# Sixteen block sums of the output weights moved from GpSimd to VectorE

## The chip, the core and the metric

The kernel runs on one core of one Trainium2 chip. The metric is the time of one execution in device microseconds (us), and lower is better. The core has five engines with a queue each: TensorE (PE in the profile, its weight loads PEld), VectorE (DVE), ScalarE (ACT), GpSimd (POOL) and SyncE (SP), which here only issues DMAs. Every engine takes its instructions in order. PSUM is the memory into which TensorE writes; GpSimd works on SBUF alone in this kernel.

## The reference

One layer of a block with two parallel branches, 1024 tokens of width 1024 and 256 context tokens, all in float32:

```python
h  = rms_norm(x, g_pre) * (1 + sc) + sh
ua, gate_a, q, k, v, gate_b, gm = split_proj(h @ w_in)
...                                   # rms norm and rotary on q and k, context keys and values appended
o  = latent_attention(q, k_all, v_all)            # 16 heads, 4 key groups, softmax over 1280 keys
y_attn = (o * silu(gate_b)) @ w_attn_out
y_conv = conv_module(ua, gate_a, ...)             # 31 taps, layer norm, silu, @ w_conv_out
out = (sigmoid(ga) * y_conv + sigmoid(gb) * y_attn) @ w_out
x_new = x + gt * rms_norm(out, g_post)
```

What matters here is the last product, `@ w_out`, a 1024 x 1024 by 1024 x 1024 product.

## The kernel before

Every float32 product is made as three products of a high and a low part (`mm3`): the high part is a cast to the tensor engine's rounded float32, the low part is the rest. `split` makes the pair, with the cast on ScalarE and the subtraction on VectorE unless other engines are named.

The two products at the end (`w_attn_out`, side 0, and `w_out`, side 1) are not made as eight block products of a 2 x 2 blocking but as seven, after Winograd's form of Strassen's method. For that the weights' blocks have to be added and subtracted first. `LEFT` and `RIGHT` list these sums: an entry `(n, i, (x, op, y))` says that operand n is made in block i, as block x plus or minus block y. `right_operands` does it for `w_out`, in four rounds t = 0 to 3. In each round it loads two row strips of 128 x 1024 into tiles of the tag `y4` (three buffers; the profile calls them `y`), so that there are four blocks of 128 x 512, b[0] to b[3], two in each tile. Five operands come of them, the entries j = 0 to 4 of `RIGHT`; the first is a plain block, the other four are sums made in place: b0 = b1 - b0, b1 = b3 - b1, b3 = b3 - b0 and b2 = b2 - b3. For each operand ScalarE casts the high part (`his`, line 664), VectorE subtracts the low part (`los`, line 656), and SP stores both to DRAM (`stores`, line 658), from where `coef_load` fetches them for the product. `RSTEPS` says in which of nine steps each of these parts is issued, and how many steps of the attention loop pass before the next.

The rounds run inside the attention loop (lines 1482 to 1515), as a generator: each turn of the loop issues one step, of some 1.9 us. In a turn TensorE makes the scores of a key block (`score`, tiles `ps`), ScalarE exponentiates them (`pe`), GpSimd adds the exponentials up into `psum`, VectorE adds every fifth pair (`part`, which GpSimd then adds to `psum`), and TensorE weighs the values (`po`, 20 products in a row). Ahead of that the row maxima of the next head pair are found: TensorE makes the scores once more in `max_pieces`, VectorE reduces them (`mx`, then `mc` in `max_cols`), TensorE transposes the result and ScalarE writes it as a row (`mr`). Score tiles, maxima tiles and transposes share five PSUM buffers. Beside all that, `filler` runs the projections in small pieces (tiles `ppj`): here those of `w_conv_out`, which VectorE evicts to `ts`.

Order: TensorE's instructions stay in the order in which they are written. Those of VectorE, ScalarE and GpSimd are held to it only until line 1435; in the attention loop a scheduler orders them by priority and by when it expects their inputs. What the generators issue is marked as urgent and, on VectorE, is put behind the newest maximum:

```python
        for g in late.pop(i, []):
            with tc.issue_after(crit[0].ins), urgent():
                d = next(g, None)
```

(`crit[0]` is the newest reduction of a maximum, an instruction of VectorE; `issue_after` orders instructions of that engine alone.)

The edge column: the convolution (`conv_taps`, long before the attention loop) copies one column at the end of `odd_end`, line 809: `V.tensor_copy(O[:, 511:512], acc[:, 1, 511:512])`.

Of the kernel before, what the change touches and what calls it, by code (L numbers as in the profile page):

```python
# [34 lines left out]
def block_kernel(ctx: ExitStack, tc: tile.TileContext, x, cx, cc, wmod, bmodT, bmodg, vecs, gpost,  # L35
# [18 lines left out]
    PE, V, S, G = (Ordered(e) for e in (nc.tensor, nc.vector, nc.scalar, nc.gpsimd))  # L54
# [11 lines left out]
    def tl(tag, shape, bufs, dtype=F32, pool="sb"):  # L66
        return pools[pool].tile(list(shape), dtype, tag=tag, bufs=bufs, name=nm(tag))
# [37 lines left out]
    def f32(ap):  # L105
        return ap.bitcast(F32)
# [537 lines left out]
    def right_operands():  # L644

        for t in range(4):
            b = []
            for r in range(2):
                y = tl("y4", (P, 2, 512), 3)
                SP.dma_start(out=y[:].rearrange("p c n -> p (c n)"), in_=wout[(t + 4 * r) * P:(t + 4 * r + 1) * P, :])  # L650
                b += [y[:, c, :] for c in range(2)]
            yield 2
            w = {}
            for n, (sums, his, los, stores, rest) in enumerate(RSTEPS):
                for j in los:
                    V.tensor_tensor(out=w[j][:, 1, :], in0=b[RIGHT[j][1]], in1=f32(w[j][:, 0, :]), op=SUB)
                for j in stores:
                    SP.dma_start(out=opD[1][RIGHT[j][0]][t][:], in_=f32(w[j][:]))
                for j in sums:
                    i, (x, op, y) = RIGHT[j][1:]  # L660
                    G.tensor_tensor(out=b[i], in0=b[x], in1=b[y], op=op)
                for j in his:
                    w[j] = tl("acc", (P, 2, 512), 2, F32R) if (5 * t + j) % 3 else tl("ysum", (P, 2, 512), 1, F32R)
                    S.copy(w[j][:, 0, :], b[RIGHT[j][1]])
                yield rest
# [473 lines left out]
    def last_split():  # L1139
        yield from z_split(1)  # L1140
        yield from right_operands()
# [481 lines left out]
```

## Time and profile before

| | us |
|---|---|
| median of 3 runs | 1394.6 |
| lowest and highest | 1391.34, 1399.88 |
| the profiled execution | 1392.78 |
| span of its instructions | 1391.0 |
| TensorE busy | 1347.2 (97%) |
| VectorE busy | 1018.9 (73%) |
| GpSimd busy | 712.7 (51%) |
| ScalarE busy | 564.6 (41%) |

The span is from the first to the last instruction; the profiled execution's own time is 1.8 us longer. A helper that keeps the program's order records most instructions, so nearly all of them carry the line 50 (L50) in the profile, and one goes by the tiles' names: `y<-y,y` is an instruction that writes a tile y and reads two tiles y. In the rows of instructions in order of time the columns are the start, the duration (both in us), the engine, the line, the operation, the tiles, the shapes and the count; in square brackets stands how long the engine had been idle before it and what ended that. In the rows by stretch, each engine's busy time (and instructions) follow one another: PE, PEld, DVE, ACT, POOL, then the granted clock of TensorE, the share of the DMA engines and GB/s.

### The profile page before, as it was taken

To read this page: it belongs to the slowest core of one execution; us is meant where nothing else is said; L and a number is where in the kernel's file an instruction comes from. 1 tells how busy PE (TensorE), PEld (TensorE's weight loads), DVE (VectorE), ACT (ScalarE), POOL (GpSimd) and SP (SyncE) were. 2 spreads that over 40 slices of the span, in tenths; PEclk is the share of its full clock that TensorE was granted. 3 is DMA by queue.
4 is the path that set the end of the run, shared out by engine and by line. 5 is a ranking of instruction groups with operands and counts; after the bars stand their busy time and mean duration, and the time that the engine had idled before them with its cause. 6 is when DMAs were issued, how large, how long until landed. Compare 5 with 4: busy or idle time off the path is not lost.

```text
span 1391.0 us, 19520 instructions
## 1 busy us (share of the span) xinstructions
PE 1347.2 (97%) x6520; PEld 999.8 (72%) x6520; DVE 1018.9 (73%) x1521; ACT 564.6 (41%) x1389; POOL 712.7 (51%) x577
## 2 busy tenths in 40 slices
PE   5999999999999999999999999999999999999995
PEld 3767898988888888666666666666666665788774
DVE  3477988897979899657765776677586676348977
ACT  5542344434353442244434444544454344122232
POOL 2121346667657562346764655566446667263623
PEclk9999999999999999999999999999999999999998
DMA  9731534544544448524544444545365567699754
GB/s 342 254 122 54 183 115 132 191 140 130 174 136 153 148 130 234 169 92 157 163 144 124 150 152 127 169 130 160 99 190 190 193 207 261 202 321 352 250 183 151
DMA packets 153333, 242.45 MB, mean 174 GB/s; under 512 B 19936, under 2 KB 72716, under 8 KB 153232
## 3 DMA queue, kind: packets, MB, share of 16 engines
q1 hardware_dynamic: 139792, 218.07, 47.4%
q10 hardware_dynamic: 13440, 23.14, 5.8%
q8 instruction: 51, 0.84, 0.3%
q14 instruction: 50, 0.41, 0.1%
HBM read 161.50 MB, written 79.52 MB: 173 GB/s over the span
## 4 chain that ended last, share of the span: by engine, by line
PE 79%; DVE 6%; DMA 5%; ACT 4%; POOL 3%; issue 2%; ACTq 1%; SPq 0%; POOLq 0%; DVEq 0%
PE ppj L50 37%; PE po L50 21%; PE ps L50 17%; PE pm L50 4%; DVE t L50 2%; DMA wm<-in_wmod 1%; ACT pe L50 1%; DVE pconv L50 1%; POOL y L50 1%; DVE mx L50 1%; DMA y<-in_wout 1%; POOL wgl L50 1%; DMA vt<-vD 1%; ACTq L50 1%; ACT ts L50 0%
## 5 line engine op out<-in xcount | busy, mean ns | idle before, releaser
L50 PE MATMUL ppj<-t,whi 128*128 128x512 f32 x1728 | 615.3, 401 | 4.4 <-DVE t L50 2.6
L50 PEld LDWEIGHTS ppj<-t,whi 128*128 128x128 f32 x1728 | 326.7, 189 | 106.7 <-issue 32.3
L50 PE MATMUL ppj<-t,wlo 128*128 128x512 f32 x864 | 340.5, 394 | 0.7 <-POOL wlo L50 0.7
L50 DVE TENSOR_REDUCE mx<-ps 128x1 f32<-128x512 f32 (+1 forms) x320 | 199.4, 683 | 104.2 <-PE ps L50 103.9
L50 ACT ACTIVATE pe<-ps 128x512 f32<-128x512 f32 x320 | 188.2, 597 | 203.5 <-PE ps L50 196.6
L50 PE MATMUL ps<-r,kk 128*128 128x512 f32 (+1 forms) x640 | 202.8, 398 | 0.7 <-DMA r<-mr 0.7
L50 POOL TENSOR_TENSOR psum<-psum,pe 128x512 f32<-128x512 f32 x128 | 173.3, 1370 | 41.3 <-ACT pe L50 37.5
L50 PEld LDWEIGHTS ppj<-t,wlo 128*128 128x128 f32 x864 | 164.0, 190 | 31.3 <-POOL wlo L50 1.8
L50 DVE SCALAR_TENSOR_TENSOR pconv<-y,cw,pconv 128x507 f32<-128x507 f32 (+5 forms) x224 | 168.0, 750 | 19.9 <-ACT pconv L50 13.7
L50 POOL TENSOR_TENSOR wlo<-wraw,whi 128x512 fp32r<-128x512 f32 x69 | 91.3, 1332 | 129.3 <-ACT whi L50 122.5
L50 PE MATMUL po<-pe,vt 128*64 128x512 f32 x640 | 144.4, 597 | 0.0
L50 POOL TENSOR_TENSOR psum<-psum,part 128x512 f32<-128x512 f32 x64 | 89.9, 1407 | 104.9 <-DVE part L50 104.9
L50 PEld LDWEIGHTS ps<-r,kk 128*128 128x128 f32 (+1 forms) x640 | 121.0, 189 | 30.3 <-DMA y<-in_wout 0.9
L50 PE MATMUL po<-wgh,t 128*128 128x384 f32 x512 | 131.7, 338 | 0.0
L50 PEld LDWEIGHTS po<-pe,vt 128*64 128x64 f32 x640 | 43.1, 136 | 81.2 <-issue 78.9
L50 PEld LDWEIGHTS po<-wgh,t 128*128 128x128 f32 x512 | 92.9, 188 | 1.3
L50 DVE SCALAR_TENSOR_TENSOR pconv<-y,cs,pconv 128x505 f32<-128x505 f32 (+7 forms) x120 | 90.0, 750 | 3.6
L50 PE MATMUL po<-wgl,t 128*128 128x384 f32 x256 | 86.3, 337 | 0.0
L50 ACT CAST whi<-wraw 128x512 fp32r<-128x512 f32 x112 | 69.2, 631 | 39.1 <-DMA wraw<-in_wch 18.3
L50 POOL TENSOR_TENSOR psum<-pe,pe 128x512 f32<-128x512 f32 x32 | 42.4, 1344 | 74.5 <-ACT pe L50 74.5
L50 DVE TENSOR_TENSOR part<-pe,pe 128x512 f32<-128x512 f32 x64 | 68.4, 1072 | 14.5 <-ACT pe L50 10.6
L50 PE MATMUL ps<-kk,rq 64*128 64x512 f32 (+1 forms) x384 | 65.8, 404 | 6.1 <-ACT pe L50 6.0
(221 smaller groups left out, 1802.4 us busy)
## 6 DMA issues: line engine op xcount, KB each, us to landing
wraw<-in_wch SPq DMA_DIRECT2D x96, 256.0 KB
opD<-opw SPq DMA_DIRECT2D x56, 256.0 KB
wm<-in_wmod SPq DMA_DIRECT2D x24, 512.0 KB
W<-opD SPq DMA_DIRECT2D x48, 256.0 KB
r1D<-r1st SPq DMA_DIRECT2D x32, 256.0 KB
y<-accD SPq DMA_DIRECT2D x16, 512.0 KB
r<-r1D ACTq DMA_DIRECT2D x32, 256.0 KB
opD<-acc SPq DMA_DIRECT2D x13, 512.0 KB
```

What stands on the lines that cost most here:

```text
L50: i = f(*a, **k)
```

## The change

The sums in `right_operands` are issued to VectorE instead of GpSimd: four in each of four rounds, each of 128 x 512 float32 with both operands in SBUF. The change is announced as "sums of the output weights' blocks made by VectorE in place of GpSimd, with the edge column's copy on VectorE"; the diff has one line.

```diff
@@ -658,7 +658,7 @@
                     SP.dma_start(out=opD[1][RIGHT[j][0]][t][:], in_=f32(w[j][:]))
                 for j in sums:
                     i, (x, op, y) = RIGHT[j][1:]
-                    G.tensor_tensor(out=b[i], in0=b[x], in1=b[y], op=op)
+                    V.tensor_tensor(out=b[i], in0=b[x], in1=b[y], op=op)
                 for j in his:
                     w[j] = tl("acc", (P, 2, 512), 2, F32R) if (5 * t + j) % 3 else tl("ysum", (P, 2, 512), 1, F32R)
                     S.copy(w[j][:, 0, :], b[RIGHT[j][1]])
```

## Prediction

> **What bounds the kernel now.** I read the page's totals and its chain first, then the tiles that the moved line writes, the busy time by stretch, and last the engines' instructions in order of time around those tiles.
>
> ```profile
> PE 1347.2 (97%) x6520; PEld 999.8 (72%) x6520; DVE 1018.9 (73%) x1521; ACT 564.6 (41%) x1389; POOL 712.7 (51%) x577
> ...
> PE 79%; DVE 6%; DMA 5%; ACT 4%; POOL 3%; issue 2%; ACTq 1%; SPq 0%; POOLq 0%; DVEq 0%
> ```
>
> TensorE (PE) is busy for 97% and holds 79% of the chain. So an edit on another engine is worth only the TensorE time that is lost to waits, and I look for that where the moved line runs. Its tiles between 1050 and 1162 us:
>
> ```profile
> L50 DVE TENSOR_TENSOR acc<-y,acc x13: 642/927/1796, 1070.2 to 1160.7; 128x512 fp32r<-128x512 f32 x13
> L50 POOL TENSOR_TENSOR y<-y x8: 1264/1292/1608, 1061.0 to 1155.3; 128x512 f32<-128x512 f32 x8
> L50 POOL TENSOR_TENSOR y<-y,y x8: 1282/1416/1747, 1062.4 to 1153.6; 128x512 f32<-128x512 f32 x8
> ```
>
> These are the 16 sums, four for each t, all inside the end of the attention loop (columns: min/median/max ns, first and last start). TensorE there (us, then busy by engine, granted clock, DMA):
>
> ```profile
> 1050.00:1100.00 50.00, 49.02 (x235) 29.70 (x234) 36.21 (x56) 21.34 (x39) 31.20 (x24) 1.00 0.58 201
> 1100.00:1120.00 20.00, 18.52 (x73) 12.28 (x75) 11.77 (x16) 8.57 (x16) 12.54 (x10) 0.91 0.60 198
> 1120.00:1160.00 40.00, 38.14 (x189) 23.29 (x185) 30.61 (x35) 18.34 (x34) 31.09 (x22) 1.00 0.59 205
> ```
>
> TensorE has holes of 0.98, 1.48 and 1.86 us in them, and in the second row the clock is 0.91. The holes one by one, from TensorE's own instructions:
>
> ```profile
> 1069.02 0.50 PE L50 MATMUL ps<-kk,rq 64*128 64x512 f32 x1 [0.98 <-ACT pe L50]
> ...
> 1108.31 0.49 PE L50 MATMUL ps<-kk,rq 64*128 64x512 f32 x1 [1.48 <-ACT pe L50]
> ...
> 1158.66 0.42 PE L50 MATMUL ps<-psum,ones 128*32 128x128 f32 x8 [0.47 <-POOL psum L50]
> 1160.33 0.43 PE L50 MATMUL ps<-psum,ones 128*32 128x128 f32 x8 [1.25 <-POOL psum L50]
> ```
>
> The first two wait for a PSUM tile that ScalarE (ACT) reads in an exponential (pe); the last two for GpSimd's softmax sum. Why is ScalarE late?
>
> ```profile
> 1062.34 0.62 ACT L50 CAST acc<-y 128x512 fp32r<-128x512 f32 x1 [5.49 <-POOL y L50]
> ...
> 1102.17 0.62 ACT L50 CAST acc<-y 128x512 fp32r<-128x512 f32 x1 [2.86 <-POOL y L50]
> ```
>
> Its casts of the sums stand in its queue ahead of exponentials, and wait for GpSimd. So the moved instructions do cost TensorE something today, twice through ScalarE's queue and once through GpSimd's.
>
> **The change part by part.** *Taken off GpSimd:* 8 x 1.29 + 8 x 1.42 = 21.7 us, by the medians above. GpSimd's order around them:
>
> ```profile
> 1061.01 1.29 POOL L50 TENSOR_TENSOR y<-y 128x512 f32<-128x512 f32 x1 [1.31 <-DVE ysum L50]
> ...
> 1100.39 3.11 POOL L50 TENSOR_TENSOR y<-y,y 128x512 f32<-128x512 f32 x2
> ...
> 1149.31 1.30 POOL L50 TENSOR_TENSOR y<-y 128x512 f32<-128x512 f32 x1 [0.63 <-DVE ysum L50]
> ...
> 1152.02 3.22 POOL L50 TENSOR_TENSOR y<-y,y 128x512 f32<-128x512 f32 x2 [0.17 <-DMA y<-in_wout]
> 1155.32 1.61 POOL L50 TENSOR_TENSOR y<-y 128x512 f32<-128x512 f32 x1
> 1156.89 3.38 POOL L50 TENSOR_TENSOR psum<-psum,part 128x512 f32<-128x512 f32 x2
> ```
>
> *Added to VectorE (DVE):* 16 sums of 128x512, two operands in SBUF. The nearest row is the subtraction of the same tiles, acc<-y,acc: 0.64 us at its shortest, 0.93 median, 1.80 longest. So 16 x 0.64 = 10.2 and 16 x 1.80 = 28.8 are the ends, and I take the median, 14.8 us. VectorE is busy for 36.21 + 11.77 + 30.61 = 78.6 of these 110 us; with the sums 93.4, so it still has room as an average. The order matters more than the share:
>
> ```profile
> 1060.26 0.68 DVE L50 TENSOR_TENSOR ysum<-y,ysum 128x512 fp32r<-128x512 f32 x1
> 1066.37 0.69 DVE L50 TENSOR_TENSOR wlo<-wraw,whi 128x512 fp32r<-128x512 f32 x1 [5.44 <-ACT whi L50]
> ...
> 1094.51 1.80 DVE L50 TENSOR_TENSOR acc<-y,acc 128x512 fp32r<-128x512 f32 x1
> 1096.22 2.47 DVE L50 TENSOR_REDUCE mx<-ps 128x1 f32<-128x512 f32 x4
> 1098.62 0.68 DVE L50 TENSOR_TENSOR O<-O,R 128x512 f32<-128x512 f32 x1
> 1099.22 0.17 DVE L50 TENSOR_REDUCE mc<-mx 128x8 f32<-128x24 f32 x1
> ...
> 1155.71 1.76 DVE L50 TENSOR_TENSOR part<-pe,pe 128x512 f32<-128x512 f32 x1
> ```
>
> *t = 0.* The first subtraction (1060.26) overwrites nothing but must be done before the first sum, which then runs at once on VectorE: it ends at 1060.94 + 0.69 = 1061.6 in place of 1061.01 + 1.29 = 1062.3, the second at 1062.3 in place of 1063.7. VectorE had 5.44 us of nothing there, which hides all four. ScalarE's two casts come 0.7 and 1.4 us earlier, and the exponential behind them too, more than the hole of 0.98: **-1.0 us.**
>
> *t = 1.* ScalarE's second cast waits until the second sum is done (the first of the pair at 1100.39, so 1102.1). On VectorE the sums follow the subtraction that ends at 1096.3, or the four maxima, O and mc that end at 1099.4; two at 0.93 end at 1098.2 or 1101.3, which is 0.8 to 3.9 us earlier. The hole of 1.48 goes: **-1.5 us.** The clock row loses 0.09 x 20 = 1.8 us behind that hole; the hole of 0.98 left the clock at 1.00, so I give half of it to chance: **-0.9 us.**
>
> *t = 2* has no hole now: 0.
>
> *t = 3.* GpSimd does three sums (1152.02 to 1156.9) and only then the last two softmax sums, on which TensorE waits 0.47 + 1.25 = 1.72. Without its own sums GpSimd is free when the parts are there. The second part ends at 1155.71 + 1.76 = 1157.5, its softmax sum at 1.29 more, 1158.8, and TensorE is ready at 1158.66 - 0.47 = 1158.2: 0.6 us stays as long as part comes no earlier. **-1.1 us.** The sum of two tiles cannot start before its load has landed (1152.02). On VectorE it now holds up what is queued behind it: a PSUM eviction, wlo and the first part. That costs part nothing at best, and at worst the time from the first sum's end to that landing, 1152.02 - 1150.61 = 1.4 us, and three sums at 0.93, 4.2 in all; I expect part no later than now, since VectorE's rows like that 1.76, beside GpSimd's sums, go back towards 0.69.
>
> *What it costs back.* Where sums come ahead of maxima, PSUM tiles come free later. Nothing in the trace shows this pair; the nearest is a TensorE hole, 0.98, the least is none, and the most is the 6.4 worked out for the first rival below. I take one such hole: **+1.0 us.** The moved line issues no DMA; the stores and loads of these tiles follow the subtractions as before.
>
> Sum: -1.0 - 1.5 - 0.9 - 1.1 + 1.0 = -3.5 us; all of the 4.2 us of holes and the 1.8 of clock gone and nothing paid, -6.0.
>
> Is it kept to the end?
>
> ```profile
> 1195.00:1320.00 125.00, 124.31 (x545) 101.78 (x543) 87.24 (x109) 30.70 (x52) 56.91 (x36) 1.00 0.85 290
> ```
>
> The only stop in that stretch:
>
> ```profile
> 1312.16 3.47 PE L50 MATMUL ps<-W,opd 128*128 128x512 f32 x14 [0.69 <-DVE opd L50]
> ```
>
> Behind the loop TensorE is busy for 124.31 of 125 us, and its one stop, 0.69 us at 1312, is for VectorE, whose inputs are TensorE's results and come earlier too. DMA at 0.85 has some room. I keep the whole. 1392.8 us is the profiled execution's own time, so 1389.3; the median of the three runs, 1394.6, lies 1.8 higher, so 1391.1 in runs.
>
> [...]
>
> **The rivals.** *VectorE becomes late (slower).* If GpSimd's adds catch the sums, three of them cost 3 x 1.80 = 5.4 us ahead of the maxima and mc. TensorE's transpose of mc has a start:
>
> ```profile
> 1103.43 0.27 PE L50 MATMUL ps<-ident,mc 128*8 128x128 f32 x1
> ```
>
> mc ends at 1099.4, so the slack is 4.0 us: from there on it decides. 5.4 - 4.0 = 1.4 us, with a clock dip of 1.8 behind it 3.2, at t = 1 and t = 2 (t = 0 has its sums behind mc): +6.4, less the 2.1 still won at t = 0 and t = 3: +4.3, so 1398.9 in runs. For it: VectorE's longest rows. Against: GpSimd has 21.7 us less to do.
>
> *Nothing is won.* Most of the 5.49 us at 1062.34 is a wait for VectorE's subtraction, which stays; casts remain in ScalarE's queue, other waits step into the holes: 0, 1394.6. For it: only 0.7 us of that wait is certain to go.
>
> *The change does half of what it says.* The edge column's copy is already VectorE's:
>
> ```profile
> L50 DVE COPY y<-pconv x8: 157/158/160, 125.8 to 544.1; 128x1 f32<-128x1 f32 x8
> ```
>
> The diff leaves it alone, so that half is 0 in any case.
>
> **How the numbers follow.** Forecast (-2 to -6) 0.50, range 1388.6 to 1392.6; nothing won (within 2) 0.27; VectorE late (+2 and more) 0.18; more than -6, by another order of the queues, 0.05. ScalarE, VectorE and GpSimd aren't held to the written order here, so a moved instruction can reorder its neighbours. The runs shown spread from 1391.34 to 1399.88, a median of three can be 3 off: 1383 to 1401 holds 8 in 10. A measurement of this kernel can tell about 1%, 14 us, from no change; the holes and the dip hold 6.0, so faster by that 0.02, slower 0.04, the rest within.
>
> **What would show it.** VectorE's list gets y<-y x8 and y<-y,y x8 of 128x512 between 1055 and 1160, at 0.7 to 1.1 us mean; GpSimd keeps eight y<-y before 560 us. The ScalarE casts wait for VectorE, under 3 us each; TensorE's holes at 1069 and 1108 and the waits for psum near 1159 are gone and the clock is 1.00. Wrong: new TensorE waits for mx, mc or mr, or sums at 1.5 us and more.

## The result and the profile after

The changed kernel takes 1386.3 us (median of 10 runs, 1382.73 to 1388.8), the kernel before 1393.59 (10 runs beside them, 1387.85 to 1399.88). The ratio is 0.9944, with a 95% interval of 0.9926 to 0.9962: 7.8 us faster, between 5.3 and 10.3. That is 0.6%, less than the 1% that the prediction took for what a measurement can tell from no change, but the interval lies clear of 1. It is also more than the forecast of 3.5: the median lies beyond its range of 2 to 6 (1388.6 to 1392.6 us), and only the near end of the interval lies within.

The page of the profile after (its execution, 1382.73 us, was the fastest of the ten), the lines with busy times and chain:

```profile
PE 1341.6 (97%) x6520; PEld 997.2 (72%) x6520; DVE 1023.7 (74%) x1537; ACT 564.0 (41%) x1389; POOL 689.3 (50%) x561
...
PE 83%; DVE 5%; DMA 4%; ACT 3%; POOL 2%; issue 2%; ACTq 0%; SPq 0%; POOLq 0%; DVEq 0%
```

Sixteen instructions went from GpSimd (577 to 561) to VectorE (1521 to 1537), and TensorE holds 83% of the chain in place of 79%. The moved sums in the view of the tiles y, after (min/median/max ns, first and last start):

```profile
L50 DVE TENSOR_TENSOR acc<-y,acc x13: 642/687/1778, 1068.5 to 1155.1; 128x512 fp32r<-128x512 f32 x13
L50 DVE TENSOR_TENSOR y<-y x8: 679/684/1382, 1058.0 to 1151.2; 128x512 f32<-128x512 f32 x8
L50 DVE TENSOR_TENSOR y<-y,y x8: 677/688/1170, 1058.7 to 1150.0; 128x512 f32<-128x512 f32 x8
```

A sum costs 0.68 to 0.69 us on VectorE where GpSimd took 1.29 to 1.42, and the subtraction acc<-y,acc next to it fell from a median of 0.93 to 0.69.

The stretches after, with the columns of the prediction's rows:

```profile
1050.00:1100.00 50.00, 49.85 (x238) 30.66 (x236) 39.03 (x62) 21.80 (x39) 26.34 (x20) 1.00 0.61 212
1100.00:1120.00 20.00, 19.45 (x99) 12.28 (x98) 12.07 (x18) 8.72 (x17) 8.07 (x7) 1.00 0.75 242
1120.00:1160.00 40.00, 40.00 (x193) 26.36 (x192) 33.61 (x44) 19.98 (x38) 22.82 (x17) 1.00 0.61 222
```

TensorE lacks 0.15 + 0.55 + 0 us here, where it lacked 0.98 + 1.48 + 1.86, and the clock is 1.00 in all three. VectorE is busy for 39.03 + 12.07 + 33.61 = 84.7 us in place of 78.6; but these windows stand at fixed times, and the changed kernel is some us further on in its program there. What is left of the holes, from TensorE's instructions in order of time:

```profile
1065.25 0.49 PE L50 MATMUL ps<-kk,rq 64*128 64x512 f32 x1 [0.15 <-ACT pe L50]
...
1103.77 0.50 PE L50 MATMUL ps<-kk,rq 64*128 64x512 f32 x1 [0.55 <-DVE mx L50]
```

ScalarE's first casts of t = 0, and VectorE's order at t = 0 and t = 1, after:

```profile
1058.74 1.35 ACT L50 CAST acc<-y 128x512 fp32r<-128x512 f32 x2 [4.85 <-DVE y L50]
```

```profile
1058.02 0.69 DVE L50 TENSOR_TENSOR y<-y 128x512 f32<-128x512 f32 x1
1058.74 1.42 DVE L50 TENSOR_TENSOR y<-y,y 128x512 f32<-128x512 f32 x2
...
1092.41 0.68 DVE L50 TENSOR_TENSOR y<-y 128x512 f32<-128x512 f32 x1
1093.01 0.69 DVE L50 TENSOR_REDUCE mx<-ps 128x2 f32<-128x512 f32 x1
1093.61 1.17 DVE L50 TENSOR_TENSOR y<-y,y 128x512 f32<-128x512 f32 x1
...
1096.50 0.17 DVE L50 TENSOR_REDUCE mc<-mx 128x8 f32<-128x24 f32 x1
...
1103.02 2.48 DVE L50 TENSOR_REDUCE mx<-ps 128x1 f32<-128x512 f32 x4 [2.63 <-PE ps L50]
```

At t = 0 the two casts run back to back (x2), where the second one waited 0.7 us more for GpSimd. At t = 1 two sums (0.68 and 1.17) stand between the maxima, but that costs TensorE nothing that can be seen: mc ends at 1096.67, and TensorE transposes it only at 1099.96. The 0.55 at 1103.77 is put down to the next maxima, which begin at 1103.02, after VectorE had been idle for 2.63 us until TensorE's scores came. VectorE was not late there; the same idle time of 2.63 stands ahead of these maxima before (at 1106.49) and with the sums left out (at 1104.12). So this wait is what is left where the longer one was, and not a price of the sums.

**A ruler for the stage.** Whole runs of one kernel differ by up to 13 us, so most of what follows is read from inside a trace. TensorE's order is the same in every kernel here. "Stage" is the time from the first group of 20 weighing products after 1050 us (po, at the head of round t = 0) to the last group of softmax sums behind round t = 3; "front" is the part up to the fourth such group (t = 0 and t = 1), "back" the rest. Before, stage and front end at these starts:

```profile
1056.75 4.51 PE L50 MATMUL po<-pe,vt 128*64 128x512 f32 x20
...
1116.95 4.51 PE L50 MATMUL po<-pe,vt 128*64 128x512 f32 x20
...
1192.31 0.65 PE L50 MATMUL ps<-psum,ones 128*32 128x128 f32 x16
```

| kernel | front | back | stage | ratio of the runs to before |
|---|---|---|---|---|
| before | 60.20 | 75.36 | 135.56 | |
| before, once more | 58.63 | 75.36 | 133.99 | |
| after | 57.07 | 72.28 | 129.35 | 0.9944 [0.9926, 0.9962] |
| after, once more | 56.73 | 72.27 | 129.00 | |
| sums on VectorE at t = 3 only | 58.64 | 73.68 | 132.32 | 0.9976 [0.9958, 0.9995] |
| sums on VectorE at t = 0, 1, 2 only | 56.96 | 76.11 | 133.07 | 0.9976 [0.9961, 0.9991] |
| no sums | 56.93 | 72.29 | 129.22 | 0.9955 [0.9934, 0.9976] |
| every sum twice on VectorE | 62.92 | 73.16 | 136.08 | 0.9997 [0.9975, 1.0019] |
| casts a step later, sums on GpSimd | 57.86 | 76.87 | 134.73 | 0.9965 [0.9946, 0.9984] |
| casts that wait for no sum, sums on GpSimd | 57.52 | 75.85 | 133.37 | 0.9986 [0.9966, 1.0006] |
| after, GpSimd loaded again | 57.42 | 73.59 | 131.01 | 0.9953 [0.9934, 0.9972] |

One run of the ten with the sums of t = 0, 1, 2 took 4658.62 us and is left out of its ratio. Front, back and stage come from one trace of each kernel. The expectations of the first four experiments below measure the stage to the projections that follow, some 0.55 us longer: their 136.1 and 129.9 are 135.56 and 129.35 here.

### The profile page after: what moved, and what is told of

It reads as the page before. It is cut to its first block, busy times and chain, and to the rows that moved or that the text cites. A ratio compares the mean times of both kernels' runs of the same rounds, so it can differ in the third digit from the quotient of the medians.

```text
span 1380.9 us, 19526 instructions
## 1 busy us (share of the span) xinstructions
PE 1341.6 (97%) x6520; PEld 997.2 (72%) x6520; DVE 1023.7 (74%) x1537; ACT 564.0 (41%) x1389; POOL 689.3 (50%) x561
## 4 chain that ended last, share of the span: by engine, by line
PE 83%; DVE 5%; DMA 4%; ACT 3%; POOL 2%; issue 2%; ACTq 0%; SPq 0%; POOLq 0%; DVEq 0%
PE ppj L50 39%; PE po L50 22%; PE ps L50 18%; PE pm L50 4%; DVE t L50 2%; DMA wm<-in_wmod 1%; DVE pconv L50 1%; POOL wgl L50 1%; DVE mx L50 1%; DMA vt<-vD 1%; ACT pe L50 1%; ACT ts L50 0%; DMA tgbD<-ts 0%; ACT y L50 0%; ACTq L50 0%
```

## Experiments

Theory A: ScalarE's casts, held by GpSimd's sums, block its in-order queue, and TensorE waits for the exponentials behind them (t = 0, t = 1); at t = 3 GpSimd itself is late with the softmax sums. The rivals: the gain comes only from GpSimd's time, or only from a dip of the clock that was there by chance, or VectorE pays part of it back.

**Both kernels again,** unchanged.

> The kernel before, unchanged, profiled once more, to see what of the stage's 135.6 us (first weighing to the last, 1056.75 to 1192.31) repeats. Holes of 0.98, 1.48 and 0.47 + 1.25 us repeat within 0.1 us if they come from the order of the queues. The dip of the clock of 1.8 us behind 1108 us is there again if the hole makes it, and comes and goes if it is chance: stage 135.6 or 133.9 us.

> The changed kernel, unchanged, profiled once more: stage 129.3 to 129.5 us with no dip of the clock, since no hole is longer than 0.6 us.

The kernel before, the row of the stretch of its second hole, and its holes:

```profile
1100.00:1120.00 20.00, 18.52 (x81) 11.60 (x79) 13.42 (x20) 9.08 (x17) 16.01 (x12) 1.00 0.51 186
```

```profile
1072.48 0.50 PE L50 MATMUL ps<-kk,rq 64*128 64x512 f32 x1 [0.94 <-ACT pe L50]
1111.77 0.50 PE L50 MATMUL ps<-kk,rq 64*128 64x512 f32 x1 [1.48 <-ACT pe L50]
...
1160.58 0.43 PE L50 MATMUL ps<-psum,ones 128*32 128x128 f32 x8 [0.68 <-POOL psum L50]
1162.25 0.43 PE L50 MATMUL ps<-psum,ones 128*32 128x128 f32 x8 [1.24 <-POOL psum L50]
```

The holes come back, three of them within 0.04 us and one, 0.47, as 0.68, which is more than the 0.1 expected. The dip of the clock does not: the same hole of 1.48 leaves it at 1.00, and the front is 1.57 us shorter for it (60.20 to 58.63). So the stage gains 133.99 - 129.00 = 5.0 us without the dip and 135.56 - 129.35 = 6.2 with it. The changed kernel repeats within 0.35 us, at 129.00 a little under what was expected.

**The sums of one part of the rounds alone.**

```diff
-                    G.tensor_tensor(out=b[i], in0=b[x], in1=b[y], op=op)
+                    (V if t == 3 else G).tensor_tensor(out=b[i], in0=b[x], in1=b[y], op=op)    # t = 3 only
+                    (G if t == 3 else V).tensor_tensor(out=b[i], in0=b[x], in1=b[y], op=op)    # t = 0, 1, 2 only
```

> VectorE makes the four sums of t = 3 alone; the other twelve stay on GpSimd. I measure the stage from the start of the weighing at 1056.8 us (before) or 1053.9 us (changed kernel) to the start of the last run of projections at 1193.0 or 1183.8 us: 136.1 us before, 129.9 us with the change. Theory A (each hole of TensorE is closed where it stands, and VectorE pays nothing): TensorE's waits for psum near 1159 us go, those at 1069 and 1108 us stay, with the clock at 0.91; stage 134.0 to 134.6 us, ratio about 0.9985. Rival B (the gain comes from another order of the queues as a whole, not from single holes): the shares don't add up, and the stage stays within 1 us of 136.1 or of 129.9 us.

> VectorE makes the twelve sums of t = 0, 1 and 2; those of t = 3 stay on GpSimd. Theory A: the holes at 1069 and 1108 us and the dip of the clock go, 4.3 us together, and TensorE's wait for psum near the end of the loop, about 1.7 us, stays; stage 131.5 to 132.2 us, ratio about 0.997. Rival B (order as a whole): no such split.

With t = 3 only, TensorE's holes:

```profile
1073.55 0.50 PE L50 MATMUL ps<-kk,rq 64*128 64x512 f32 x1 [0.94 <-ACT pe L50]
1112.85 0.50 PE L50 MATMUL ps<-kk,rq 64*128 64x512 f32 x1 [1.48 <-ACT pe L50]
...
1161.65 0.42 PE L50 MATMUL ps<-psum,ones 128*32 128x128 f32 x8 [0.39 <-POOL psum L50]
```

Both front holes stay, the two for psum shrink from 1.92 to 0.39, and the back gains 75.36 - 73.68 = 1.68 us. The front has no dip here either (58.64, as in the repeat), which is why the stage missed what was expected. With t = 0 to 2 only, the front is that of the changed kernel (56.96), and the hole for psum is there and larger:

```profile
1156.86 0.42 PE L50 MATMUL ps<-psum,ones 128*32 128x128 f32 x8 [2.08 <-POOL psum L50]
```

```profile
1150.00:1160.00 10.00, 7.92 (x44) 3.77 (x45) 8.51 (x7) 4.24 (x8) 8.42 (x6) 0.89 0.63 240
```

The clock dips behind it, and the stage, 133.6 by the longer measure, came out 1.4 above the top of what was expected. So the front is won by the sums of t = 0 to 2 and the softmax wait by those of t = 3, and the runs agree: 0.9976 x 0.9976 = 0.9952, against 0.9944 for both. In the traces the two shares don't simply add: against the repeat of before they are 1.67 and 0.92, together 2.6, where both gain 5.0. The rest is the dip and the larger hole with t = 0 to 2 only, and 0.6 at t = 3 that needs both (below).

**No sums.** The line is left out.

```diff
-                    G.tensor_tensor(out=b[i], in0=b[x], in1=b[y], op=op)
+                    pass
```

> The sixteen sums are left out altogether, so the casts and subtractions that follow take the plain blocks and the last product is not the reference's. This is the floor of what the sums can cost. Theory A (VectorE makes them for nothing): stage within 0.7 us of the changed kernel's 129.9 us, ratio 0.993 to 0.997. Rival C (VectorE pays for them about the 1.0 us of the prediction, or more, in late maxima, and the gain on GpSimd's side is larger by that): stage 129.0 us or less, ratio lower than the changed kernel's by 0.0007 or more.

The stage is 129.22, the changed kernel's 129.35 and 129.00: in sum, the sums on VectorE cost TensorE nothing that a stage shows. The 0.55 for mx at t = 1 is gone without them, and the time from the third weighing to the fourth is 18.11 in place of 18.93 (the repeat of after). But the time from the second to the third is 20.25 in place of 19.26, with another hole in it:

```profile
1083.90 0.50 PE L50 MATMUL ps<-kk,rq 64*128 64x512 f32 x1 [0.51 <-ACT pe L50]
```

**Every sum twice on VectorE.**

```diff
-                    G.tensor_tensor(out=b[i], in0=b[x], in1=b[y], op=op)
+                    for _ in range(2):
+                        V.tensor_tensor(out=b[i], in0=b[x], in1=b[y], op=op)
```

> VectorE makes each of the sixteen sums twice over in place (the second time on the block already summed, so the last product is not the reference's): 16 more instructions of 0.68 us, 11 us of VectorE in the stage. Theory A (VectorE has room there): stage 129.9 to 131.5 us, new TensorE waits for the maxima of under 1.5 us in sum. Rival C (VectorE's place ahead of the maxima is what costs): waits for mx or mc and a dip of the clock come back, stage 133 us or more.

```profile
1074.41 0.49 PE L50 MATMUL ps<-kk,rq 64*128 64x512 f32 x1 [1.54 <-DVE mx L50]
...
1115.86 0.49 PE L50 MATMUL ps<-kk,rq 64*128 64x512 f32 x1 [1.40 <-ACT pe L50]
```

```profile
1060.00:1080.00 20.00, 18.46 (x77) 11.54 (x76) 18.14 (x25) 8.03 (x15) 9.67 (x7) 0.91 0.34 112
...
1100.00:1120.00 20.00, 18.61 (x77) 11.65 (x76) 18.99 (x27) 7.67 (x15) 12.10 (x8) 0.91 0.34 124
```

VectorE is busy for 18.14 and 18.99 us of 20, and a dip of the clock follows both holes. At the first it is late with the maxima, which start without any idle time before them. At the second TensorE waits for an exponential: ahead of it in ScalarE's queue stands a cast that waited 1.66 us for VectorE's second pass, so VectorE is now the slow producer of theory A. The stage is 6.7 to 7.1 us longer than with the sums once, nearly all of it in the front (5.9 to 6.2). So theory A's "VectorE has room" ends somewhere between one load and two, and the prediction's slower rival, late maxima, is a true mechanism of this kernel at twice the load. This trace is of the slowest of the ten runs (1401.86, their median 1393.8).

**The casts a step later.** GpSimd keeps its sums, and the casts of j = 1 to 4 move one step down in `RSTEPS`.

```diff
-    ((4,), (1,), (), (), 2), ((), (2,), (1,), (), 2), ...
+    ((4,), (), (), (), 2), ((), (1,), (), (), 2), ((), (2,), (1,), (), 2), ...
```

> The sums stay on GpSimd, all sixteen; only ScalarE's casts of the four summed blocks (and what follows from them) are issued one step, two turns of the loop, later, so that they find the sums done. Each round is thereby two turns, some 3.8 us, longer, and the sums of t = 3 come some 11 us later than before. Theory A (at t = 0 and t = 1 TensorE waits because casts that wait for GpSimd stand ahead of exponentials in ScalarE's queue): ScalarE's waits for GpSimd's y fall from 15.8 us to under 5, TensorE's waits for pe from 2.5 us to under 1; from the first weighing of the stage to the fourth 58.0 to 59.0 us, against 60.2 before and 57.1 with the change. Rival D (it is GpSimd's time itself: its adds of the exponentials come late and keep their buffers): the holes of 0.98 and 1.48 us stay. Neither says what happens to the hole behind t = 3, whose place shifts.

ScalarE's waits between 1050 and 1165 us (total, times, longest):

```profile
ACT acc L50 <- POOL y L50: 13.7, 7, 5.5
...
ACT ysum L50 <- POOL y L50: 9.0, 3, 5.5
```

These waits were to go and rose, from 15.8 (11.3 + 4.5) to 22.7 us: the casts stand right behind the sums again (the first of t = 0 waits 5.47 us). The hole of 0.94 stayed, that of 1.48 became 0.87, and at t = 3 TensorE waited 2.86 for psum. The edit did not do what it was for, so it tells nothing between the theories. Its runs are faster by 0.35% all the same, which its one trace, with a stage of 134.73, does not explain.

**Casts that wait for no sum.** GpSimd keeps its sums, and the casts of j = 1 to 4 read a tile that has long been there.

```diff
-                    S.copy(w[j][:, 0, :], b[RIGHT[j][1]])
+                    S.copy(w[j][:, 0, :], f32(zt[0][0][0][:]) if j else b[0])
```

> The sums stay on GpSimd, all sixteen, but ScalarE's casts of the four summed blocks read another tile that has long been ready, so they wait for no sum (the last product is not the reference's); GpSimd's work and VectorE's are as before. Theory A (casts that wait for GpSimd hold up the exponentials behind them): TensorE's holes of 0.98 and 1.48 us shrink to 0.3 us or less; from the first weighing of the stage to the fourth 56.7 to 57.5 us (58.6 before, without a dip of the clock; 56.7 to 57.1 with the change). The hole behind t = 3, which is GpSimd's own, stays: from the fourth weighing to the last 74.5 us or more (75.4 before, 72.3 with the change). Rival D (GpSimd's time holds the exponentials' buffers): the holes stay, 58.4 us or more.

```profile
1071.90 0.50 PE L50 MATMUL ps<-kk,rq 64*128 64x512 f32 x1 [0.15 <-ACT pe L50]
...
1110.89 0.49 PE L50 MATMUL ps<-kk,rq 64*128 64x512 f32 x1 [0.30 <-ACT pe L50]
...
1153.97 0.47 PE L50 MATMUL ps<-r,kk 65*128 65x512 f32 x1 [1.51 <-DMA r<-mr]
...
1161.85 0.42 PE L50 MATMUL ps<-psum,ones 128*32 128x128 f32 x8 [1.25 <-POOL psum L50]
```

GpSimd does as much as before, and still the front holes fall from 0.94 and 1.48 to 0.15 and 0.30, and the front to 57.52, at the edge of what theory A expected (another hole of 0.50 stands at 1090 us). So at t = 0 and t = 1 it is ScalarE's queue and not GpSimd's time. At t = 3 holes for psum stay, and the back is 75.85. This separates the two halves of the theory.

One more thing stands in that queue. Before, at t = 1:

```profile
1106.31 1.30 ACTq L50 DMA_DIRECT2D r<-mr  x2
1107.66 1.09 ACT L50 ACTIVATE pe<-ps 128x512 f32<-128x512 f32 x2 [1.38 <-PE ps L50]
```

The exponential that TensorE waits for is put down to TensorE's scores, but by TensorE's rows the last of these was done at 1106.02. For 1.30 us ScalarE's queue issues the DMA of the row of maxima, and only then comes the exponential. The late casts push that issue into TensorE's way; after, it has ended (at 1102.29) before the last of the scores are done. Whether that DMA, issued from another queue, would have closed the hole too is untested.

**GpSimd loaded again.** The changed kernel, with an idle add of 128 x 480 on GpSimd for each sum.

```diff
                     V.tensor_tensor(out=b[i], in0=b[x], in1=b[y], op=op)
+                    o = b[i][:, 0:480]
+                    G.tensor_tensor(out=tl("idle", (P, 480), 1, pool="B")[:], in0=o, in1=o, op=op)
```

> The changed kernel, with GpSimd making, behind each of VectorE's sixteen sums, one more of 128x480 from its result into a tile that nobody reads: GpSimd has about its old load again, but ScalarE waits for VectorE alone. Theory A: the holes of t = 0 and t = 1 stay closed (first weighing to the fourth 56.7 to 57.6 us), and the one behind t = 3 comes back, for GpSimd's last softmax sums stand behind the added instructions (fourth to last 73.5 us or more). Rival D: both come back, 58.4 us or more for the first part. Rival E (VectorE only keeps its time while GpSimd leaves the tiles alone): VectorE's sums take 1.5 us and more, new waits for maxima of 1 us and more.

```profile
L50 POOL TENSOR_TENSOR idle<-y x16: 981/1314/1494, 1064.4 to 1161.3; 128x480 f32<-128x480 f32 x16
...
L50 DVE TENSOR_TENSOR y<-y x8: 679/783/1470, 1063.7 to 1159.7; 128x512 f32<-128x512 f32 x8
L50 DVE TENSOR_TENSOR y<-y,y x8: 691/1372/1739, 1064.4 to 1157.7; 128x512 f32<-128x512 f32 x8
```

Beside GpSimd's adds the second kind of sum doubles on VectorE, 0.69 to 1.37 us; that median is under the 1.5 of rival E, and no wait for maxima beyond the 0.55 came. The front gives back only 0.35 to 0.7 us (57.42), the back 1.3 (73.59). That is the expected size, but not in the expected place: no wait for psum came back, TensorE waits 0.70 for an exponential (pe) behind t = 3 instead. By the groups, 1.0 of the 1.3 stands behind t = 3 and 0.3 at t = 2. GpSimd is as busy in this stage as before (93.4 us against 93.2), and still 3.0 of the 5.0 us stay won. So GpSimd's load itself costs about 1 us behind t = 3; that the order of the softmax sums alone is the reason is not shown.

## Why the prediction was right, and where its sizes were off

The direction, the place and the mechanism held; the stage gave 5.0 to 6.2 us where the sum said 3.5. The size did not hold: the runs' 7.8 lies in the row "more than -6, by another order of the queues", which had a chance of 0.05. In the first pair of traces 1.6 of the stage's 6.2 is the clock, which comes by chance; without it the sum said 2.6 and the stage gave 5.0. By its steps:

- **t = 0, -1.0:** right. The hole of 0.94 to 0.98 became 0.15; the interval between its weighing groups is 0.82 us shorter between the two repeats.
- **t = 1, -1.5:** the hole for pe went, but a wait of 0.55 for mx was left in its place; the interval gives 1.09.
- **Clock, -0.9, as half a chance:** fair. Of the three traces that keep the hole of 1.48 it dips in one, and costs 1.57 us there. It was no part of the gain between the repeats.
- **t = 2, 0:** "has no hole now" was misread. The row from 1120 to 1160 lacks 1.86 us, and 0.47 of it is neither of the two holes for psum:

```profile
1152.09 0.47 PE L50 MATMUL ps<-r,kk 65*128 65x512 f32 x1 [0.47 <-DMA r<-mr]
```

Between the repeats, the two intervals from the fourth to the sixth group are 0.38 and 0.50 us shorter. The second is this wait for the row of maxima: before, ScalarE writes it 2.5 us after TensorE's transpose starts (1144.61 to 1147.12), behind a cast that waited 1.33 us to start; after, 0.8 us (1138.16 to 1138.92). The first is one run of score pieces just ahead of the fifth group, in the repeat of before and of after:

```profile
1137.46 1.11 PE L50 MATMUL ps<-kk,rq 64*128 64x512 f32 x6
...
1133.22 0.73 PE L50 MATMUL ps<-kk,rq 64*128 64x512 f32 x6
```

What these pieces wait for no row names. Both gains are there with t = 0 to 2 only (19.25 and 16.39 us, as in the changed kernel).
- **t = 3, -1.1 with 0.6 left over:** under-sized, and the largest error of the sum. Nothing is left, the two holes of 1.92 are gone, and the interval gives 2.21. The step that failed is that the sums hold up the parts and "part comes no earlier". GpSimd's last two adds, after, in its order of time, and VectorE's order around them:

```profile
1145.67 1.59 POOL L50 TENSOR_TENSOR psum<-psum,part 128x512 f32<-128x512 f32 x1 [2.50 <-DVE part L50]
1147.96 1.59 POOL L50 TENSOR_TENSOR psum<-psum,part 128x512 f32<-128x512 f32 x1 [0.69 <-DVE part L50]
```

```profile
1144.85 0.68 DVE L50 TENSOR_TENSOR part<-pe,pe 128x512 f32<-128x512 f32 x1
1145.45 0.68 DVE L50 TENSOR_TENSOR y<-y 128x512 f32<-128x512 f32 x1
1146.05 1.77 DVE L50 TENSOR_TENSOR part<-pe,pe 128x512 f32<-128x512 f32 x1
1147.74 0.68 DVE L50 TENSOR_TENSOR y<-y,y 128x512 f32<-128x512 f32 x1
```

Now it is GpSimd that waits for part, 2.50 and 0.69 us, where it was still at its own sums before, and it ends at 1149.6, before TensorE needs the sum. One sum stands between the two parts and three stand behind them, so no load holds a part up. The first part went back from 1.78 to 0.68 as foreseen, but the second still takes 1.77, beside GpSimd's softmax add. It comes earlier by its place: it ends 1.3 us behind the start of the sixth weighing, before 3.8. With t = 3 only, the order is the one that the prediction assumed: two sums wait for their load (2.14 us of VectorE) ahead of both parts, the second part ends at 3.5, and 0.39 of the wait for psum stays, near the 0.6 of the sum.

- **Back cost, +1.0:** about 0. A wait for mx appeared, as the text had it under "wrong", of 0.55, but VectorE had been idle ahead of those maxima, and the kernel without sums has no shorter stage.
- **VectorE's price, 14.8 us:** the median of a row beside GpSimd's sums (0.93) was taken for sums that leave fewer of GpSimd's instructions beside them (561 in place of 577); at 0.68 to 0.69 the 16 medians make 11.0. VectorE's busy time in the stage rose by 4.9 in the first pair of traces and 6.3 in the second (87.66 to 92.59, 87.80 to 94.08).
- **Casts under 3 us each:** wrong for one, 4.85 at t = 0. Most of it is the wait for the subtraction ahead, as the rival "nothing is won" had it; the 0.7 us that were certain were enough for the hole. In all, ScalarE waited 11.8 and 13.2 us for y in the two traces, in place of 15.8.
- **Kept to the end:** right, 5.0 and 6.2 of the stage arrive. TensorE's last stop at the back, 0.69 for opd, became 0.41 to 0.43.

The rival "VectorE late" fell because its price did not come: its three sums at 1.80 were to eat 4.0 us of slack, and at t = 1 the four took 0.68 to 1.17. "Nothing is won" falls by the interval, 5.3 to 10.3. That the edge column's half adds nothing holds, as the diff has no line for it.

The two pairs of traces differ by more than the stage: by 10.1 us in the first (spans of 1391.0 and 1380.9) and 7.9 in the second (1392.6 and 1384.7). Of that, 0.9 and 0.6 lie behind the stage, and 3.0 and 2.3 ahead of it. Ahead of it no line differs, and the loop's first weighing starts anywhere from 593.4 to 600.3 us in the eleven traces, without regard to the kernel; so I take that for chance. The interval's near end, 5.3, fits the stage. A difference of its own ahead of the stage is neither shown nor excluded.

## What to carry to other kernels

When the bound engine has short holes, follow each to the engine that releases it and then one place up that engine's queue: here casts that waited up to 5.49 us for GpSimd held up the exponentials behind them, and TensorE's holes of 0.94 to 0.98 and 1.48 us fell to 0.15 and 0.30 once those casts waited for no sum. Moving the producer to an engine with room cured that, as long as the room lasted: 16 sums cost nothing that could be seen (a stage of 129.35 us, 129.22 without them), and 32 all that had been won (136.08, where the two traces of before have 135.56 and 133.99). Price a two-operand add on VectorE by what GpSimd will do beside it after the change, not by the rows of before: the sum of two tiles (y<-y,y) had a median of 0.69 us without GpSimd's sums and 1.37 beside its added instructions.

## What was not expected of the hardware

**A hole's length alone does not decide whether the clock dips.** In the stage, of six holes of 1.40 to 1.54 us, three were followed by a granted clock of 0.91 over their 20 us (before, and both of the doubled sums), and three by 1.00 (the repeat of before, t = 3 only, and the free casts' 1.51). Both longer holes, 2.08 and 2.86, had a dip (0.89 in the row of the first; 0.86 over the ten microseconds from 1160 us in the other), and the holes of 0.94 to 1.25 read here had none. But far ahead of the stage, between 682 and 690 us, every one of the eleven traces has a hole of 1.47 to 1.50, and the clock dips behind it in all eleven, to 0.83 over ten microseconds in ten of them. Just ahead of the stage, two of 1.76 had a dip, and one of 1.47 (GpSimd loaded again) had none. The first kind, before:

```profile
685.73 0.50 PE L50 MATMUL ps<-kk,rq 64*128 64x512 f32 x1 [1.50 <-ACT pe L50]
```

So it is a chance in the stage and none at that place; what makes the difference no run here shows.

**Work taken off GpSimd shortens VectorE's own work.** From the first to the last group of the stage, before, after, and with the sums left out, VectorE's busy time is the third figure behind the length:

```profile
1056.75:1192.31 135.56, 130.92 (x607) 81.39 (x605) 87.66 (x111) 56.87 (x104) 93.17 (x67) 0.99 0.63 216
...
1053.80:1183.15 129.35, 128.65 (x608) 80.27 (x606) 92.59 (x127) 57.03 (x104) 70.31 (x51) 1.00 0.66 226
...
1054.21:1183.43 129.22, 128.56 (x607) 80.26 (x605) 80.15 (x111) 55.87 (x102) 69.02 (x51) 1.00 0.66 226
```

The same 111 instructions of VectorE take 87.66 us beside GpSimd's sums and 80.15 without them, so making the sums on GpSimd cost VectorE 7.5 us as it was. Its subtractions fell from 0.93 to 0.69; with GpSimd loaded again the sums y<-y,y rose from 0.69 to 1.37, y<-y to 0.78, and VectorE's busy time to 103.02. That rows become shorter without GpSimd's sums the prediction used at t = 3 alone, and not in the price of the sums. What makes them longer beside GpSimd's work no run here shows.
